# Scores of two attention groups as three fp32r products of high parts and rests, in an encoder layer on one core

## The chip, the cores and the metric

The kernel runs on one core of one Trainium2 chip. The metric is the device time of one execution in microseconds. The kernel before takes 909.24 us, the median of three runs (908.89, 909.24 and 909.37).

## What is computed

One encoder layer over 512 positions of width 1024: a LayerNorm, a mixer of two groups of attention heads, a cross attention to a memory of 256 rows, and a gated feed-forward block, each followed by a residual sum and a LayerNorm. The change touches the mixer only. Cut to it, the reference reads:

```python
def banded_attention(q, k, v, n_side, sink=None):
    ...
    s = jnp.einsum('bnqhgd,bnkhd->bnhgqk', qb, kw).astype(jnp.float32) * (dh ** -0.5)
    ...
    p = jnp.where(mask, jnp.exp(s - m[..., None]), 0.0)
    ...
def parallel_mixer(h, positions, w_in, attn_sink, g_win, g_dil, w_out):
    z = h @ w_in
    qa, ka, va, qb, kb, vb = jnp.split(z, SPLITS, axis=-1)
    qa = partial_rope(qa...); ka = partial_rope(ka...)
    out_a, _ = banded_attention(qa, ka, va, WIN_HALF, attn_sink.reshape(WIN_KV_HEADS, -1))
    ...
    for gi, (window, dil) in enumerate(DIL_PAIRS):
        o, lse = banded_attention(to_residue(qb[:, :, gi], dil), to_residue(kb[:, :, gi], dil), ...)
```

The eight **sink heads** (`qa`, `ka`, `va`) have a window of 128 on each side, an extra sink logit, and only two key heads. The second group has eight heads in each of three dilations (`DIL_PAIRS` is (128, 1), (512, 4), (2048, 16)); its member with dilation 1 is the **undilated group**. Every head is 64 wide, so a score product contracts over 64 rows.

## The kernel before

**Products.** All large products take fp32 data apart: a high part, which is the number cast to fp32r by ScalarE (ACT), and a rest, which VectorE (DVE) gets by subtracting the high part from the number. TensorE (PE) then adds three products, high by high, high by rest and rest by high. `wsplit` (lines 134 to 142) does that for a block of weights: the cast is L136, the subtraction L138. The scores of the mixer are the exception. They are products of plain fp32 numbers, which PE takes in two passes, so that each shows as two records in the trace.

**Two heads at once.** A tile of queries or keys holds two heads, on partitions 0 to 63 and 64 to 127 (`HJ`). Score products are issued for the two heads in turn, `j` = 0 and 1; each uses one half of the rows of PE's array.

**Projections.** `proj` makes 512 positions of two heads: 24 matmuls of 512 columns into a PSUM tile `g` (`chunk_fm`), then the rotation (`rope`, lines 525 to 531). That is a product (L528) and a shuffle (L529) on DVE, then a product (L530) and a sum (L531) on GpSimd (POOL). The sum writes the tile of queries or keys, in fp32. Such tiles come from a pool of 12 buffers of 2 KB a partition (tag `x`).

**Items.** The attention itself runs as items between the projections. `item_a(c)` is the undilated group for heads 2c and 2c+1 (called A0 to A3 here), `item_w(c)` the sink heads (W0 to W3), `item_b(c)` the other two dilations (B0 to B3). An item issues its score products on PE, then for each block and head a masked minimum on DVE (L725, L771 or L815) and an exponential on ACT (L728, L774 or L819), both in that order on their engines. It pauses, transposes the probabilities on PE (L682), lets ACT copy them out of PSUM (L687), pauses, and multiplies them by the values (L694).

**Order.** PE's order is the program's own (`manual_schedule`): a counter `now` goes up by one for each matmul of a projection (`mmt`, `tick`), and an item goes on once its keys and queries are `ready` and its pause is over. `proj` sets `ready` to `now + LAG`, and `LAG` is 24 matmuls. Item A's transposes come 18 matmuls behind its scores. If no buffer of the pool is free, `x_tile` forces the next item. The order of ACT, DVE and POOL is set by the compiler's scheduler when the kernel is built. Each engine then works through its own list in that order.

Of the kernel before, what the change touches and what calls it, by code (L numbers as in the profile page):

```python
# [9 lines left out]
F32 = mybir.dt.float32  # L10
F32R = mybir.dt.float32r
I32 = mybir.dt.int32
AF = mybir.ActivationFunctionType
ALU = mybir.AluOpType
# [3 lines left out]
P = 128  # L18
D = 1024
S = 512  # L20
# [17 lines left out]
QA, KA, VA, QB, KB, VB = 0, 512, 640, 768, 2304, 3840  # L38
# [34 lines left out]
def hymba_layer(ctx: ExitStack, tc: tile.TileContext, A, cst_d, out):  # L73
    nc = tc.nc
# [11 lines left out]
    xpool = ctx.enter_context(pool("x2k", side="right"))  # L86
# [3 lines left out]
    rope = [cpool.tile([P, S], F32, tag="rope", bufs=2, name=n) for n in ("rc", "rsn")]  # L90
# [43 lines left out]
    def split(raw, shape, hp, htag, hb, lp, ltag, lb, eng=None):  # L134
        hi = hp.tile(shape, F32R, tag=htag, bufs=hb, name="hi")
        nc.scalar.copy(hi, raw)  # L136
        lo = lp.tile(shape, F32R, tag=ltag, bufs=lb, name="lo")
        (eng or nc.vector).tensor_tensor(lo, raw, hi.bitcast(F32), ALU.subtract)  # L138
        return hi, lo
# [4 lines left out]
    def w_cols(w, c0, eng=None):  # L144
        raw = wpool.tile([P, KD, P], F32, tag="raw", bufs=3, name="raw")
        nc.sync.dma_start(raw, w.rearrange("(k p) f -> p k f", p=P)[:, :, c0 : c0 + P])
        return wsplit(raw, [P, KD, P], eng)
# [19 lines left out]
    def mm(o, l, r, first, last):  # L167
        on_pe(nc.tensor.matmul(o, l, r, start=first, stop=last))  # L168
# [91 lines left out]
    def v_raw(i):  # L260
        src = w_in[2 * i * P : (2 * i + 2) * P, VB : VB + 512].rearrange("(k p) f -> p k f", p=P)
        if i < 3:
            raw = [wpool.tile([P, 2, 512], F32, tag="raw", bufs=3, name="raw")]
            nc.sync.dma_start(raw[0], src)
        else:
            raw = [xpool.tile([P, 1, 512], F32, tag="x", bufs=12, name="raw") for _ in range(2)]
            for k in range(2):
                nc.sync.dma_start(raw[k], src[:, k : k + 1, :])
        wv0.append([raw, [wpool.tile([P, 2, 512], F32R, tag=n, bufs=6, name=n) for n in ("hi", "lo")]])
# [255 lines left out]
    def rope(ps, view, dest):  # L525
        rn[0] += 1
        zc, sh = zs[:, rn[0] % 2, :], zs[:, 2 + rn[0] % 2, :]
        nc.vector.tensor_tensor(zc, ps, rc, ALU.mult)  # L528
        nc.vector.stream_shuffle(sh, ps, SWAP)  # L529
        nc.gpsimd.tensor_tensor(sh, sh, rsn, ALU.mult)  # L530
        nc.gpsimd.tensor_tensor(view[1](dest), view[0](zc), view[0](sh), ALU.add)  # L531
# [8 lines left out]
    m2 = cst[:, CM1 + 64 : CM1 + 192]  # L540
    mB = cst[:, CM1 : CM1 + 384].rearrange("p (a b) -> p a b", b=192)[:, :, 64:192]
    mA = cst[:, CMA : CMA + 384]
    ka = p1.tile([P, S], F32, name="ka")
    sq = ka
    va = p1.tile([P, NB, P], F32, name="va")
    Q = {}
    V = {0: vt}
# [31 lines left out]
        while any(q[0] == name for q in queue):  # L579
            force()  # L580

    XB = 12

    def x_tile(shape, dt, key):
        while sum(e[1] for e in held) >= XB:
            force()
        t = xpool.tile(shape, dt, tag="x", bufs=XB, name="x")
        held.append([key, True])
        return t

    def x_free(*keys):
        for e in held:
            if e[0] in keys:
                e[1] = False

    def mmt(o, l, r, first, last, w=1.0):
        mm(o, l, r, first, last)
# [12 lines left out]

    def proj(key, wt, view, dest=None):
        ps = chunk_fm(key, wt)
        if dest is None:
            dest = Q[key] = x_tile([P, S], F32, key)
        rope(ps, view, dest)
        ready[key] = now[0] + LAG

    def proj_b(n, g, c):
        wt = first.pop(n) if g == c == 0 else w_cols(w_in, (KB if n == "k" else QB) + g * 512 + c * P)
# [71 lines left out]
    def pv(o, parts):  # L691
        for i, (t0, t1, lhs, rhs) in enumerate(parts):
            for j in range(2):
                nc.tensor.matmul(  # L694
                    o[HJ[j], t0:t1], lhs(j), rhs(j), start=i == 0, stop=i == len(parts) - 1
                )

    def item_a(c):
        k, q = Q["k", 0, c], Q["q", 0, c]
        s = [s_tile() for _ in range(2)]  # L700
        cols = ((0, 0), (0, 128), (1, 0), (1, 256))
        for q0, o0, kk0 in ((0, 0, 0), (448, 64, 384)):
            for j in range(2):
                mm(s[j][o0 : o0 + 64, 0, 0:P], q[HJ[j], q0 : q0 + 64], k[HJ[j], kk0 : kk0 + P], True, True)
        for u in range(1, 4):
            bk, c0 = cols[u]
            for j in range(2):
                mm(
                    s[j][:, bk, c0 : c0 + 256],
                    q[HJ[j], 128 * u - 64 : 128 * u + 64],  # L710
                    k[HJ[j], 128 * (u - 1) : 128 * (u + 1)],
                    True,
                    True,
                )
        x_free(("k", 0, c), ("q", 0, c))
        pus = []
        for u in range(4):
            nk = 256 if u else P
            bk, c0 = cols[u]
            pu = p2.tile([P, 2, nk], F32, tag="p", bufs=4, name="pu")  # L720
            pus.append(pu)
            for j in range(2):
                h_ = 2 * c + j
                ng, dn = (stT[:, i, u, h_ : h_ + 1] for i in (0, 1))
                nc.vector.tensor_tensor_reduce(  # L725
                    pu[:, j, :], s[j][:, bk, c0 : c0 + nk], m1 if u else m2, SCALE, 3.0e38, ALU.add, ALU.min, ng
                )
                nc.scalar.activation(pu[:, j, :], pu[:, j, :], AF.Exp, bias=ng, scale=-1.0, accum_out=dn)  # L728
        yield 18
        lo = [pu[:, j, 0:P] for pu in pus for j in range(2)]  # L730
        up = [pu[:, j, P : 2 * P] for pu in pus[1:] for j in range(2)]
        t1, t2, t3, t4 = transposes(
            lo[0:4], [up[0], lo[4], up[1], lo[5]], [up[2], lo[6], up[3], lo[7]], [up[4], up[5]]
        )
        yield 13
        yield from meet()
        o = ps_tile("o", 1)

        def vj(kb):
            return lambda j: vt[:, kb, c * P + j * HD : c * P + (j + 1) * HD]  # L740

        pv(
            o,
            [
                (0, 64, vj(0), lambda j: t1[:, j, 0:64]),
                (64, 192, vj(0), lambda j: t1[:, 2 + j, :]),
                (192, 448, vj(2), lambda j: t3[:, 2 * j : 2 * j + 2, :]),
                (64, 320, vj(1), lambda j: t2[:, 2 * j : 2 * j + 2, :]),
                (320, 448, vj(3), lambda j: t4[:, j, :]),
                (448, 512, vj(3), lambda j: t1[:, j, 64:128]),  # L750
            ],
        )
        nc.scalar.copy(oA[:, c, :], o)

    def item_b(c, then=None):
# [35 lines left out]
        pv(o, [(u * P, (u + 1) * P, vj(g, u), pj(g, u)) for u in range(4) for g in (1, 2)])  # L791
        nc.scalar.copy(oB[:, c, :].rearrange("p (i r) -> p r i", r=4), o.rearrange("p (r i) -> p r i", r=4))

    def item_w(c, then=None):
        q = Q["w", c]
        st = spool.tile([P, NB, 2], F32, tag="ast", bufs=2, name="ast")
# [5 lines left out]
        pu4 = [p2.tile([P, 2, 386], F32, tag="p", bufs=4, name="pu") for _ in range(NB)]  # L802
        for b in (0, 3, 1, 2):
            k0, k1 = max(0, b - 1) * P, min(NB, b + 2) * P
            for j in range(2):
                mm(sc[b][j][:, 0 : k1 - k0], q[HJ[j], b * P : (b + 1) * P], ka[HJ[j], k0:k1], True, True)
        x_free(("w", c))
        for b in (0, 3, 1, 2):
            nk = (min(NB, b + 2) - max(0, b - 1)) * P
# [60 lines left out]
        nc.vector.tensor_tensor(oW[:, c, :], o, fw, ALU.mult)  # L870
        if c < 3:
            return
        for i in range(4):
            if i == 0:
                nc.scalar.activation(sq, oW[:, i, :], AF.Square)
            else:
                tmp = p2.tile([P, S], F32, tag="p", bufs=4, name="tmp")
                nc.scalar.activation(tmp, oW[:, i, :], AF.Square)
                nc.vector.tensor_tensor(sq, sq, tmp, ALU.add)
# [38 lines left out]
    def rms_scale(sq_, name):  # L918
        ps = ps_tile("o", 1, [P, NB, 2])
        for b in range(NB):  # L920
            mm(ps[:, b, :], sq_[:, b * P : (b + 1) * P], ones, True, True)
        ra = spool.tile([P, NB], F32, tag=name, bufs=1, name=name)
        nc.vector.tensor_scalar(ra, ps[:, :, 0], 1.0 / 512, EPS, ALU.mult, ALU.add)
        nc.gpsimd.tensor_tensor(ra, ra, mhalf.to_broadcast([P, NB]), ALU.pow)
        return ra
# [10 lines left out]
    with tc.manual_schedule(engines={nc.tensor.engine}):  # L936
# [6 lines left out]
        proj_b("k", 0, 0)  # L943
        proj_b("q", 0, 0)
        add("A0", keys_a(0), item_a(0))
        proj(("ka",), w_cols(w_in, KA), NAT, ka)
        proj_va()
        add("W0", [("w", 0), ("ka",)], item_w(0))
        proj_w(0)
# [36 lines left out]
        def item_c():  # L986
# [25 lines left out]
            tp = ps_tile("t", 1, [P, 4, P])  # L1012
            for u in range(4):
                nc.tensor.transpose(tp[:, u, :], stw[:, u].rearrange("p n h -> p (n h)"), ident)
            hp["w"] = rms_scale(sq, "raw_")
            for c in range(4):
                split_gain(mT, c, oW[:, c, :], gwc[:, c : c + 1])
            xw, rr = (cs.tile([8, 2, S], F32, tag="n4", bufs=2, name=n) for n in ("xw", "rr"))
# [356 lines left out]

    def t_parts(n, i, r):
        if n < 3:
            hl = [xpool.tile([P, 2, HT], F32R, tag="x", bufs=12, name="x") for _ in range(2)]
        else:
            hl = [two_k(t4, i), cpool.tile([P, 2, HT], F32R, tag="rope", bufs=2, name="t4l")]  # L1380
        nc.scalar.copy(hl[0], r)
        nc.vector.tensor_tensor(hl[1], r, hl[0].bitcast(F32), ALU.subtract)
        T.setdefault(n, []).append(hl)
# [101 lines left out]
    with gs:  # L1485
# [18 lines left out]

        def down_ops(k):
            w = w_rows(A["w_down"][0], k, 1, 0, D)
            a = split(act[:, k, :], [P, S], xpool, "x", 12, xpool, "x", 12)
            return w, a

        for k in range(KO):  # L1510
# [78 lines left out]
```

## Time and profile before

| what | before |
|---|---|
| median of three runs | 909.24 us |
| the profiled execution | 910.02 us |
| its span, first to last instruction | 908.2 us |
| around the span | 1.8 us |
| granted TensorE clock | 0.998 |
| PE busy | 896.0 us (99%) |
| DVE, ACT, POOL busy | 562.1, 385.5, 127.3 us |
| the mixer's projections and items | from about 41 to 340 us of the span |

A row of the timeline gives start and length in microseconds, engine, line and operation, the tile written and the tiles read, and in square brackets how long the engine sat idle before it and what ended that. A row of the chain of waits gives start and length of a stretch that belongs to the chain which ended last. Lengths on PE contain the way through the array, so the time that a matmul takes in a row of others is read from start to start.

### The profile page before, as it was taken

How to read it: one execution, taken by the hardware profiler on the slowest of the kernel's cores; microseconds unless marked ns; L12 is line 12 of the kernel's file. 1: busy time of each engine (PE TensorE's matmuls, PEld its weight loads, DVE VectorE, ACT ScalarE, POOL GpSimd, SP SyncE). 2: the span in 40 equal slices, each digit the busy share in tenths (PEclk: the TensorE clock that was granted, in tenths of full speed). 3: DMA queues.
4: the chain of work that ended last, by engine and by line, in shares of the span. 5: the costliest groups of instructions: out<-in, count | busy, mean ns of one | idle time of the engine just before them, and what ended most of it. 6: DMA issues, size and time to landing. Idle time of an engine off the chain costs nothing.

```text
span 908.2 us, 12950 instructions
## 1 busy us (share of the span) xinstructions
PE 896.0 (99%) x5115; PEld 768.8 (85%) x5115; DVE 562.1 (62%) x963; ACT 385.5 (42%) x672; POOL 127.3 (14%) x106
## 2 busy tenths in 40 slices
PE   8999999999999999999999999999999999999996
PEld 6778987898878798788988889899999999888885
DVE  6975145335446767869366576977777767433357
ACT  4573436415546576415454224444444445222210
POOL 1064033431443420010000010000000000000001
PEclk9999999999999999999999999999999999999999
DMA  6762041224221338415222304333333354223201
GB/s 218 224 216 70 24 140 47 71 69 117 70 71 47 93 109 237 142 47 167 89 70 70 90 26 121 91 93 93 97 112 93 95 161 140 93 94 102 83 23 70
DMA packets 117086, 92.84 MB, mean 102 GB/s; under 512 B 12488, under 2 KB 101024, under 8 KB 117026
## 3 DMA queue, kind: packets, MB, share of 16 engines
q1 hardware_dynamic: 116192, 89.80, 32.7%
q10 hardware_dynamic: 834, 2.22, 0.6%
q8 instruction: 40, 0.66, 0.3%
q14 instruction: 20, 0.16, 0.1%
HBM read 87.82 MB, written 4.19 MB: 101 GB/s over the span
## 4 chain that ended last, share of the span: by engine, by line
PE 95%; DVE 3%; DMA 1%; issue 0%; ACT 0%; POOL 0%; DVEq 0%; ACTq 0%
PE g L168 53%; PE s L168 25%; PE o L168 5%; PE t L168 4%; PE o L694 3%; PE s L682 2%; PE s L208 1%; DMA vt<-in_ln_in_g_dram 1%; PE s L1225 0%; DVE lo L282 0%; DVE oA L348 0%; DVE st L312 0%; DVE Tlo L367 0%; POOL zs L530 0%; DVE mx L1206 0%
## 5 line engine op out<-in xcount | busy, mean ns | idle before, releaser
L138 DVE TENSOR_TENSOR lo<-raw,hi 128x1024 fp32r<-128x1024 f32 x126 | 157.3, 1249 | 87.8 <-ACT hi L136 87.1
L136 ACT CAST hi<-raw 128x1024 fp32r<-128x1024 f32 x126 | 132.3, 1050 | 141.1 <-PE g L168 92.5
L168 PE MATMUL g<-Thi,hi 128*128 128x512 f32 x240 | 94.8, 395 | 0.0
L168 PE MATMUL g<-Tlo,hi 128*128 128x512 f32 x240 | 94.3, 393 | 0.0
L168 PE MATMUL g<-Thi,lo 128*128 128x512 f32 x240 | 94.0, 392 | 0.0
L109 POOL TENSOR_TENSOR rs<-ve,mhalf 128x1 f32<-128x1 f32 x18 | 15.3, 853 | 523.5 <-DVE ve L115 512.2
L530 POOL TENSOR_TENSOR zs<-zs,rsn 128x512 f32<-128x512 f32 x29 | 59.2, 2041 | 147.5 <-DVE zs L529 147.5
L168 PE MATMUL g<-Uhi,hi 128*128 128x512 f32 (+1 forms) x216 | 74.3, 344 | 0.0
L168 PE MATMUL g<-Ulo,hi 128*128 128x512 f32 (+1 forms) x216 | 74.0, 342 | 0.0
L168 PE MATMUL g<-Uhi,lo 128*128 128x512 f32 (+1 forms) x216 | 73.9, 342 | 0.0
L168 PE MATMUL g<-hi,Thi 128*128 128x512 f32 x184 | 71.6, 399 | 0.0
L168 PE MATMUL g<-hi,Tlo 128*128 128x512 f32 x184 | 71.0, 395 | 0.5 <-DVE Tlo L1173 0.5
L168 PE MATMUL g<-lo,Thi 128*128 128x512 f32 x184 | 70.6, 395 | 0.4 <-DVE lo L282 0.4
L528 DVE TENSOR_TENSOR zs<-g,rc 128x512 f32<-128x512 f32 x29 | 20.0, 688 | 68.5 <-PE g L168 31.7
L168 PE MATMUL g<-x,hi 128*128 128x256 f32 x320 | 58.8, 284 | 0.0
L168 PEld LDWEIGHTS g<-Thi,hi 128*128 128x128 f32 x240 | 45.1, 188 | 11.0 <-issue 0.9
L168 PEld LDWEIGHTS g<-Tlo,hi 128*128 128x128 f32 x240 | 45.1, 188 | 10.3 <-issue 1.4
L168 PEld LDWEIGHTS g<-Thi,lo 128*128 128x128 f32 x240 | 45.1, 188 | 9.3
L168 PEld LDWEIGHTS g<-x,hi 128*128 128x128 f32 x320 | 50.0, 192 | 0.5 <-issue 0.3
L168 PE MATMUL s<-Uhi,hi 128*128 128x512 f32 (+1 forms) x136 | 49.5, 364 | 0.0
L168 PE MATMUL s<-Ulo,hi 128*128 128x512 f32 (+1 forms) x136 | 49.5, 364 | 0.0
L168 PE MATMUL s<-Uhi,lo 128*128 128x512 f32 (+1 forms) x136 | 49.5, 364 | 0.0
(369 smaller groups left out, 2059.5 us busy)
## 6 DMA issues: line engine op xcount, KB each, us to landing
raw<-in_w_in_dram SPq DMA_DIRECT2D x37, 512.0 KB, 3.7
raw<-in_w_gate_dram SPq DMA_DIRECT2D x22, 512.0 KB, 3.8
raw<-in_w_up_dram SPq DMA_DIRECT2D x22, 512.0 KB, 3.9
raw<-in_w_down_dram SPq DMA_DIRECT2D x22, 512.0 KB, 3.4
raw<-in_w_xk_dram SPq DMA_DIRECT2D x8, 512.0 KB, 3.9
raw<-in_w_xv_dram SPq DMA_DIRECT2D x8, 512.0 KB, 3.5
raw<-in_w_xq_dram SPq DMA_DIRECT2D x8, 512.0 KB, 4.5
raw<-in_w_xo_dram SPq DMA_DIRECT2D x8, 512.0 KB, 3.5
```

The costliest lines, as they stand in the source:

```text
L109: nc.gpsimd.tensor_tensor(out_, in_, mhalf, ALU.pow)
L136: nc.scalar.copy(hi, raw)
L138: (eng or nc.vector).tensor_tensor(lo, raw, hi.bitcast(F32), ALU.subtract)
L168: on_pe(nc.tensor.matmul(o, l, r, start=first, stop=last))
L208: on_pe(nc.tensor.transpose(ps[:, i // 4, f : f + P], t[:, i * P : (i + 1) * P], ident))
L528: nc.vector.tensor_tensor(zc, ps, rc, ALU.mult)
L530: nc.gpsimd.tensor_tensor(sh, sh, rsn, ALU.mult)
L682: nc.tensor.transpose(tp[:, k, :], s_, ident)
L694: nc.tensor.matmul(o[HJ[j], t0:t1], lhs(j), rhs(j), start=i == 0, stop=i == len(parts) - 1)
```

## The change

The queries and keys of the sink heads and of the undilated group (13 projections: k and q of A0 to A3, the sink heads' key tile `ka`, and the four sink query tiles) are taken apart, as weights are. The new `in_parts` does it: ACT casts the rotated tile to a high part (new L600), DVE subtracts it for the rest (new L601). The new `scores` adds three fp32r products where one fp32 product stood. For these projections `ready` is 8 matmuls later. Each now holds two tiles instead of one, and one more while it is taken apart, so the pool has 18 buffers; to make room, the scratch for dynamic DMAs is set to 1 KB. At the edges of the sequence, item A issued two products of 64 queries each, which lay side by side in one PSUM tile. It now issues a product of 128 queries (384 to 511), of which the first 64 rows are then written over by a product of 64 queries (0 to 63). The other dilations (item B) keep their fp32 scores.

```diff
-    ka = p1.tile([P, S], F32, name="ka")
-    sq = ka
+    kfill = p1.tile([P, 32], F32, name="kfill")
+    kaT = [p1.tile([P, S], F32R, tag=n, bufs=1, name=n) for n in ("kah", "kal")]
...
-    XB = 12
+    XB = 18
...
+    PAIRS = ((0, 0), (0, 1), (1, 0))
+
+    def in_parts(raw, hl):
+
+        nc.scalar.copy(hl[0], raw)
+        nc.vector.tensor_tensor(hl[1], raw, hl[0].bitcast(F32), ALU.subtract)
...
     def proj(key, wt, view, dest=None):
         ps = chunk_fm(key, wt)
-        if dest is None:
-            dest = Q[key] = x_tile([P, S], F32, key)
-        rope(ps, view, dest)
-        ready[key] = now[0] + LAG
+        if view is RES:
+            Q[key] = x_tile([P, S], F32, key)
+            rope(ps, view, Q[key])
+            ready[key] = now[0] + LAG
+            return
+        raw = x_tile([P, S], F32, "raw")
+        rope(ps, view, raw)
+        Q[key] = dest or [x_tile([P, S], F32R, key) for _ in range(2)]
+        in_parts(raw, Q[key])
+        x_free("raw")
+        ready[key] = now[0] + LAG + 8
...
+    def scores(out_, q, q0, q1, k, k0, k1):
+        for i, (m, n) in enumerate(PAIRS):
+            for j in range(2):
+                mm(out_[j], q[m][HJ[j], q0:q1], k[n][HJ[j], k0:k1], i == 0, i == 2)
...
-        for q0, o0, kk0 in ((0, 0, 0), (448, 64, 384)):
-            for j in range(2):
-                mm(s[j][o0 : o0 + 64, 0, 0:P], q[HJ[j], q0 : q0 + 64], k[HJ[j], kk0 : kk0 + P], True, True)
+        scores([s[j][:, 0, 0:P] for j in range(2)], q, 384, 512, k, 384, 512)
+        scores([s[j][0:64, 0, 0:P] for j in range(2)], q, 0, 64, k, 0, P)
         for u in range(1, 4):
             bk, c0 = cols[u]
...
+            scores([s[j][:, bk, c0 : c0 + 256] for j in range(2)], q, 128 * u - 64, 128 * u + 64, k, 128 * (u - 1), 128 * (u + 1))
...
-            for j in range(2):
-                mm(sc[b][j][:, 0 : k1 - k0], q[HJ[j], b * P : (b + 1) * P], ka[HJ[j], k0:k1], True, True)
+            scores([sc[b][j][:, 0 : k1 - k0] for j in range(2)], q, b * P, (b + 1) * P, kaT, k0, k1)
...
-    nc = bacc.Bacc("TRN2", target_bir_lowering=False, num_devices=1)
+    nc = bacc.Bacc("TRN2", target_bir_lowering=False, num_devices=1, dynamic_dma_scratch_size=1024)
```

The rest of the diff gives the pool its 18 buffers where later stages take tiles of it, and puts the sum of squares `sq`, which used the memory of `ka`, into that of `kah`.

The scheduler lays the new work on ACT and DVE between the old. First place: ACT around A0, the first item. Before, four casts of weights (`hi`) stand ahead of the load of the table for exponentials and A0's first exponential (L728):

```order
L136 CAST hi<-raw 128x1024
L372 DMA h_dram<-oW 128x1024
L136 CAST hi<-raw 128x1024 x2
L728 ACT_TABLE_LOAD
L728 ACTIVATE pu,stT<-pu,stT 128x128
L728 ACTIVATE pu,stT<-pu,stT 128x256 x3
```

Now, with the high parts of k and q of A0 (both `x`) and of the sink heads' keys (`kah`); A0's exponentials are L739:

```order
L136 CAST hi<-raw 128x1024
L372 DMA h_dram<-oW 128x1024
L600 CAST x<-x 128x512
L136 CAST hi<-raw 128x1024
L600 CAST x<-x 128x512
L136 CAST hi<-raw 128x1024
L600 CAST kah<-x 128x512
L739 ACT_TABLE_LOAD
L739 ACTIVATE pu,stT<-pu,stT 128x128
L739 ACTIVATE pu,stT<-pu,stT 128x256
```

The cast of `kah`, which A0 does not read, stands ahead of the table load and of all of A0's exponentials.

Second place: DVE at the same point. Before, from the shuffle of A0's q on, the rotation of `ka` (the second L528) follows with only a weights' rest ahead of it:

```order
L529 STREAM_SHUFFLE zs<-g 128x512
L138 TENSOR_TENSOR lo<-raw,hi 128x1024
L528 TENSOR_TENSOR zs<-g,rc 128x512
L529 STREAM_SHUFFLE zs<-g 128x512
L138 TENSOR_TENSOR lo<-raw,hi 128x1024
L725 ISA pu,stT<-s,cst 128x128
```

Now the rests of k and q (L601) stand between:

```order
L529 STREAM_SHUFFLE zs<-g 128x512
L601 TENSOR_TENSOR x<-x 128x512
L138 TENSOR_TENSOR lo<-raw,hi 128x1024
L601 TENSOR_TENSOR x<-x 128x512
L528 TENSOR_TENSOR zs<-g,rc 128x512
L529 STREAM_SHUFFLE zs<-g 128x512
L138 TENSOR_TENSOR lo<-raw,hi 128x1024
L736 ISA pu,stT<-s,cst 128x128
```

So the rotation of `ka` begins behind the rest of q.

Third place: DVE around B1, where the sink queries of W3 have just been projected. Before, the rotation (L528, L529), a weights' rest, the scaling of W2's result (L870) and B1's first masked minimum (L771):

```order
L528 TENSOR_TENSOR zs<-g,rc 128x512
L529 STREAM_SHUFFLE zs<-g 128x512
L138 TENSOR_TENSOR lo<-raw,hi 128x1024
L870 TENSOR_TENSOR oW<-o,fw 128x512
L771 ISA pu,stT<-s,cst 128x256
```

Now, with the same steps under their new line numbers:

```order
L528 TENSOR_TENSOR zs<-g,rc 128x512
L529 STREAM_SHUFFLE zs<-g 128x512
L138 TENSOR_TENSOR lo<-raw,hi 128x1024
L882 TENSOR_TENSOR oW<-o,fw 128x512
L601 TENSOR_TENSOR x<-x 128x512
L782 ISA pu,stT<-s,cst 128x256
```

The rest of W3's queries, which B1 does not read, stands ahead of B1's minima; on ACT its cast stands likewise ahead of B1's exponentials.

More of the change, by code (lines that the diff above doesn't have):

```diff
@@ L265, in v_raw @@
         else:
-            raw = [xpool.tile([P, 1, 512], F32, tag="x", bufs=12, name="raw") for _ in range(2)]
+            raw = [xpool.tile([P, 1, 512], F32, tag="x", bufs=18, name="raw") for _ in range(2)]
             for k in range(2):
@@ L701, in item_a @@
         cols = ((0, 0), (0, 128), (1, 0), (1, 256))
-        for q0, o0, kk0 in ((0, 0, 0), (448, 64, 384)):
-            for j in range(2):
-                mm(s[j][o0 : o0 + 64, 0, 0:P], q[HJ[j], q0 : q0 + 64], k[HJ[j], kk0 : kk0 + P], True, True)
+        scores([s[j][:, 0, 0:P] for j in range(2)], q, 384, 512, k, 384, 512)
+        scores([s[j][0:64, 0, 0:P] for j in range(2)], q, 0, 64, k, 0, P)
         for u in range(1, 4):
             bk, c0 = cols[u]
-            for j in range(2):
[L708 to L714, printed above, removed]
+            scores([s[j][:, bk, c0 : c0 + 256] for j in range(2)], q, 128 * u - 64, 128 * u + 64, k, 128 * (u - 1), 128 * (u + 1))
         x_free(("k", 0, c), ("q", 0, c))
@@ L792, in item_b @@
         nc.scalar.copy(oB[:, c, :].rearrange("p (i r) -> p r i", r=4), o.rearrange("p (r i) -> p r i", r=4))
+    sq_ = []
     def item_w(c, then=None):
@@ L804, in item_w @@
             k0, k1 = max(0, b - 1) * P, min(NB, b + 2) * P
-            for j in range(2):
-                mm(sc[b][j][:, 0 : k1 - k0], q[HJ[j], b * P : (b + 1) * P], ka[HJ[j], k0:k1], True, True)
+            scores([sc[b][j][:, 0 : k1 - k0] for j in range(2)], q, b * P, (b + 1) * P, kaT, k0, k1)
         x_free(("w", c))
@@ L872, in item_w @@
             return
+        sq = p1.tile([P, S], F32, tag="kah", bufs=1, name="sq")
+        sq_.append(sq)
         for i in range(4):
@@ L945, in hymba_layer @@
         add("A0", keys_a(0), item_a(0))
-        proj(("ka",), w_cols(w_in, KA), NAT, ka)
+        proj(("ka",), w_cols(w_in, KA), NAT, kaT)
         proj_va()
@@ L1014, in item_c @@
                 nc.tensor.transpose(tp[:, u, :], stw[:, u].rearrange("p n h -> p (n h)"), ident)
-            hp["w"] = rms_scale(sq, "raw_")
+            hp["w"] = rms_scale(sq_[0], "raw_")
             for c in range(4):
@@ L1377, in t_parts @@
         if n < 3:
-            hl = [xpool.tile([P, 2, HT], F32R, tag="x", bufs=12, name="x") for _ in range(2)]
+            hl = [xpool.tile([P, 2, HT], F32R, tag="x", bufs=18, name="x") for _ in range(2)]
         else:
@@ L1506, in down_ops @@
             w = w_rows(A["w_down"][0], k, 1, 0, D)
-            a = split(act[:, k, :], [P, S], xpool, "x", 12, xpool, "x", 12)
+            a = split(act[:, k, :], [P, S], xpool, "x", 18, xpool, "x", 18)
             return w, a
```

## The prediction

> **What bounds the kernel now.** I read the page's busy times and the shares of the chain of waits first.
>
> ```profile
> PE 896.0 (99%) x5115; PEld 768.8 (85%) x5115; DVE 562.1 (62%) x963; ACT 385.5 (42%) x672; POOL 127.3 (14%) x106
> q1 hardware_dynamic: 116192, 89.80, 32.7%
> PE 95%; DVE 3%; DMA 1%; issue 0%; ACT 0%; POOL 0%; DVEq 0%; ACTq 0%
> ```
>
> PE is the bound: 95% of the chain is its own. Two things can then move the time: PE's own work, and new gaps in it. A gap of 1 us on PE between 41 and 340 us costs 1 us, because behind it PE is busy to the end.
>
> Next I read the chain in order of time, around the items.
>
> ```profile
> 57.10 1.95 PE s L168 x20
> 59.05 4.31 PE g L168 x18
> 63.36 1.53 PE s L682 x14
> ...
> 149.61 1.71 PE s L168 x12
> 151.96 7.94 PE g L168 x34
> ...
> 212.38 1.99 PE s L168 x32
> ...
> 257.13 1.99 PE s L168 x32
> 259.12 4.35 PE g L168 x18
> 263.47 1.75 PE s L682 x16
> ...
> 401.38 5.44 PE g L168 x24
> ...
> 425.84 5.76 PE g L168 x48
> ```
>
> The first three rows are A0: scores, 18 matmuls of a projection, 14 transposes in 1.53 us, 0.109 each. 149.61 is W1 (part of its scores go to other tiles, so its time is up to 151.96, 2.35 us), 212.38 and 257.13 are B0 and B1. The last two rows are plain fp32r streams: 0.227 us a matmul of 512 columns and 0.120 of 256.
>
> **PE's own work.** How long an fp32 score takes stands in the timeline of W0.
>
> ```profile
> 81.00 0.48 PE L168 MATMUL t<-ka,x 64*128 64x384 f32 x1
> 81.00 0.48 PE L168 MATMUL o<-ka,x 64*128 64x384 f32 x1
> 81.32 0.48 PE L168 MATMUL t<-ka,x 64*128 64x384 f32 x1
> ```
>
> The two heads start together (`t` and `o`), and the second pass 0.32 us later. So a step, both heads side by side, takes 0.32 at 384 columns, and by columns 0.215 at 256. W has two pairs of each width in two passes: 4 x 0.215 + 4 x 0.32 = 2.14. The other 0.21 of its 2.35 go to changing the array's shape, and stay. After: three fp32r products in place of two passes. From 0.120 and 0.227, 384 columns take 0.174; 6 x 0.120 + 6 x 0.174 = 1.76. W saves 0.38, four of them 1.5.
>
> A's three inner blocks take 3 x 2 x 0.215 = 1.29 now and 9 x 0.120 = 1.08 after. Its edges are four matmuls of 128 columns that run four at a time in two passes. A step of 128 columns takes (1.99 - 0.21) / 16 = 0.111 in B0, so the edges take 0.22. After: 3 steps for 128 queries, 3 for 64. No row shows fp32r at 128 columns; between half of 0.120 and all of it, I take 0.112 for the first (nearest: the same width in fp32) and 0.09 for the second, 0.61 together, and 0.1 for one more change of shape (bounds 0 and 0.21). Edges +0.49, inner blocks -0.21: +0.28, four of them +1.1. PE's own work: -1.5 + 1.1 = **-0.4 us**. Bounds: with 0.113 and 0.170 per step, half-price edges and no shape change, -2.3; with full-price edges and 0.21, +0.5.
>
> All this supposes that fp32r products of two heads also run side by side. In the trace fp32r runs on all 128 rows or, for `sel`, on one half only. I take the nearest row, the fp32 pair above, and keep the opposite as a rival. The Trainium skill, "TensorEngine Tiling (Array Packing)", Tiling Modes, says that tiles on different rows work independently, and that a change of tiling mode drains the array: by the first the sum is the -0.4, against it the rival's +13.4; by the second the extra shape change in A is paid in full, +0.4 in all. The trace agrees for fp32; no row shows fp32r.
>
> **Thirteen casts and thirteen rests.** They have the shape of these groups:
>
> ```profile
> L138 DVE TENSOR_TENSOR lo<-act,hi 128x512 fp32r<-128x512 f32 x22 | 14.8, 689 | 50.6 <-ACT hi L136 50.6
> L136 ACT CAST hi<-act 128x512 fp32r<-128x512 f32 x22 | 13.4, 622 | 62.5 <-PE s L168 62.4
> ```
>
> 13 x 0.62 = 8.1 us on ACT and 13 x 0.69 = 9.0 on DVE, engines that are busy 42% and 62%. Their lengths cost nothing; their places in the lists do. An item's exponentials can stand behind a cast that waits for a rotation which the item does not need. Here is A0: ACT, DVE and POOL.
>
> ```profile
> 56.66 1.05 ACT L136 CAST hi<-raw 128x1024 fp32r<-128x1024 f32 x1 [4.39 <-PE g L168]
> 57.72 1.28 ACT L728 ACT_TABLE_LOAD   x1
> 59.63 0.40 ACT L728 ACTIVATE pu<-pu,stT 128x128 f32<-128x128 f32 x1 [0.62 <-DVE stT L725]
> ...
> 62.88 0.49 ACT L728 ACTIVATE pu<-pu,stT 128x256 f32<-128x256 f32 x1
> ```
>
> ```profile
> 56.94 0.69 DVE L528 TENSOR_TENSOR zs<-g,rc 128x512 f32<-128x512 f32 x1 [2.40 <-issue]
> ```
>
> ```profile
> 55.76 1.28 POOL L531 TENSOR_TENSOR x<-zs 128x512 f32<-128x512 f32 x1
> 58.36 2.18 POOL L530 TENSOR_TENSOR zs<-zs,rsn 128x512 f32<-128x512 f32 x1 [1.32 <-DVE zs L529]
> 60.62 1.29 POOL L531 TENSOR_TENSOR ka<-zs 128x512 f32<-128x512 f32 x1
> ```
>
> The exponentials take 62.88 + 0.49 - 59.63 = 3.74 and end at 63.37, just as the transposes begin at 63.36: **no slack**. Step by step, after:
>
> - q's sum on POOL ends at 57.04; cast +0.62 and rest +0.69 with two handovers: 58.4.
> - The rotation of `ka`, at 56.94 before, stands behind that rest on DVE and starts at about 58.4, 1.45 later. So its sum on POOL ends at 61.91 + 1.45 = 63.4.
> - The cast of `kah` ends at 64.0, the table load at 65.3, the last exponential at 69.05.
> - PE: 8 matmuls more ahead of A0 are 1.8 us, so A0 starts about 58.55 (its wait for POOL in 57.10, some 0.3 us, goes) and takes 1.95 + 0.28; then 4.31 of projection: transposes from 65.1, to 66.6 if nothing held them. The last three need the last exponential: 69.05 + 0.33 = 69.4.
>
> PE stands still for **2.8 us**. If POOL's product runs in 1.3 us instead of 2.18, it is 1.9; if its sum is as slow as its product, 3.7.
>
> The same at B1:
>
> ```profile
> 254.92 0.69 DVE L528 TENSOR_TENSOR zs<-g,rc 128x512 f32<-128x512 f32 x1 [2.98 <-POOL x L531]
> ...
> 259.15 0.42 DVE L771 CUSTOM_DVE_ANT_1 pu<-s,cst 128x256 f32<-128x256 f32 x1 [1.18 <-PE s L168]
> ```
>
> ```profile
> 258.58 1.28 POOL L531 TENSOR_TENSOR x<-zs 128x512 f32<-128x512 f32 x1
> ```
>
> ```profile
> 259.68 0.51 ACT L774 ACTIVATE pu<-pu,stT 128x256 f32<-128x256 f32 x1 [4.00 <-DVE stT L771]
> ...
> 263.14 0.49 ACT L774 ACTIVATE pu<-pu,stT 128x256 f32<-128x256 f32 x1
> ```
>
> W3's rotation ends on POOL at 259.86; cast and rest end at 261.2, and only then do B1's minima start, 2.05 later than 259.15. The last exponential ends at 263.63 + 2.05 = 265.7, the transposes behind it at 266.0 instead of 263.47 + 1.75 = 265.2: **0.8 us** (0 to 1.9).
>
> W0 and W1 have more room: their exponentials are followed by a copy (L831) that PE needs at L845.
>
> ```profile
> 87.19 0.62 ACT L831 COPY x<-rd 128x512 f32<-128x512 f32 x1 [0.27 <-DVE rd L829]
> ```
>
> ```profile
> 92.05 0.44 PE o L845 x4
> ```
>
> That is 4.2 us of room. The cast of the next q now stands ahead of this copy, and its rotation ends only some 11 us behind W's start at 79.4; with cast and copy 12.2, against 92.05 - 79.4 = 12.7, less the 0.38 saved. Together with A2, whose minima are cut by one rest, I take **0.4 us** (0 to 1.0). Weight casts that now stand behind a cast of queries lose up to 3 us; the 4.39 of idle time at 56.66 says that they come that far ahead of PE's need, so this costs nothing. SP's and ACT's DMAs move with them, under the same cover. Only hardware queues appear among the DMAs, q1 with 89.80 MB above all, and DMA is 1% of the chain, at its start; so I price the smaller scratch and the six more buffers at nothing. Later stages keep PE's order.
>
> The Trainium skill, "TensorE: Matmul & The Clock Gate", opening table, gives ScalarE and VectorE a queue of 8 that is strictly first in, first out. By this rule the 2.8 and 0.8 are due; if ACT could take an exponential past a waiting cast they would be 0, and the sum -0.3. The trace agrees: the cast at 56.66 waits 4.39 us, and the table load behind it, which needs nothing, starts only at 57.72.
>
> **The sum.** -0.4 for PE's work, -0.3 for the wait ahead of A0, +2.8, +0.8 and +0.4 for the gaps: +3.3. On the profiled execution, 910.02, it gives 913.3; on the median of the runs, 909.24, which is 0.8 lower, **912.5 us**.
>
> **The rivals.**
> - *No pairs.* fp32r products of two heads run one after the other. W takes 12 x 0.120 + 12 x 0.174 = 3.53 against 2.14, A 18 x 0.120 and 6 x 0.112 + 6 x 0.09 + 0.1 against 1.51: (1.39 + 1.96) x 4 = 13.4. A0's exponentials then get 1.7 us more time, so the gaps are 2.3. 909.24 + 13.4 + 2.3 - 0.3 = 924.6. For it: no row shows fp32r on both halves. Against: fp32 starts both in the same hundredth of a microsecond (81.00), on the same halves. Chance 0.13.
> - *fp32r at 128 columns is as slow as fp32*, two passes of 0.111: A's edges take 6 x 0.222 instead of 0.61, +0.7 four times: 915.4. No row speaks against it. Chance 0.10.
> - *No gaps: not slower.* The place is the cast of `kah`. If the rotation of `ka` is done by the time A0's scores end, the exponentials start as early relative to the transposes as before, and a B1 that is as lucky loses nothing either. Then -0.7 is left, 908.5; with the low end of PE's work 906.6. It decides where POOL's sum for `ka` ends before about 60.6 (2.8 us earlier than I reckon). For it: POOL's pace varies (2.18 and 1.28 for like work). Against: the order on ACT and the time at which `ka`'s projection ends on PE, 56.9. Chance 0.20.
> - *The change doing less than it says* is not to be had: the new products and casts are in the lists. What is left, 0.07, is spread on both sides.
>
> **How the numbers follow.** The forecast has 0.50. Its own bounds: PE -2.3 to +0.5, gaps 1.9 to 6.6, less 0.3: 908.5 to 916.0. The range takes in the 128-column rival and most of the rival without gaps: **908.4 to 916.5**. Left out are the pairless case and tails, about 0.19. Chances, with 0.2% (1.8 us) about what a measurement of this kernel can tell from no change: slower, 0.45 of the forecast's 0.50, 0.13 and 0.10: 0.68. Same: 0.05 of the forecast, 0.13 of the gapless case, 0.03 of the rest: 0.21. Faster: 0.11.
>
> **What would show it.** On the chain, a row of DVE, ACT or POOL between A0's scores and its transposes, and ACT's table load near 65 instead of 57.7. In the timeline of W0, two heads' fp32r records starting together, with steps near 0.120 and 0.174, W some 0.4 shorter and A some 0.3 longer. B1's minima some 1.3 to 2 us behind its scores. I am wrong if heads start one after the other, if A's transposes follow 4.3 us behind its scores, or if PE gets gaps behind 340 us.

## The result, and the profile after

| what | before | after |
|---|---|---|
| median, six runs of each side by side | 909.59 us | 914.19 us |
| the profiled execution | 910.02 us | 914.18 us |
| its span | 908.2 us | 912.4 us |
| granted TensorE clock | 0.998 | 0.997 |

The change makes the kernel slower by 4.6 us: the ratio is 1.0054, with a 95% interval from 1.0041 to 1.0066. The prediction was 912.5 us, slower, with a range from 908.4 to 916.5.

The page of the changed kernel, busy times and shares of the chain of waits:

```profile
PE 898.5 (98%) x5187; PEld 772.2 (85%) x5187; DVE 575.5 (63%) x976; ACT 390.9 (43%) x685; POOL 124.6 (14%) x106
PE 85%; DVE 6%; POOL 3%; ACT 3%; issue 2%; DMA 1%; DVEq 0%; ACTq 0%; POOLq 0%
```

PE's share of the chain fell from 95% to 85%. The other engines' work that now stands in it isn't all lost time, since the chain can pass through an engine while PE is busy beside it. The lost time is where PE stands still. Here is the chain in order of time (start, length, what) around A0:

```profile
57.01 0.68 DVE x L601
57.69 0.54 DVE zs L528
...
59.03 2.19 POOL zs L530
...
61.29 1.29 POOL x L531
...
62.61 0.62 ACT kah L600
...
63.25 1.28 ACT L739
...
64.54 1.04 ACT pu L739 x5
...
65.73 0.69 ACT pu L739 x3
...
66.46 2.87 PE s L696 x11
```

Read it backwards from the transposes (L696): they wait for A0's exponentials, these for the load of ACT's table, this for the cast of `kah`, this for the rotation of `ka` on POOL and DVE, and the rotation for the rest of q. A0's transposes need neither `kah` nor `ka`.

DVE's list has the same pattern. The rest of `kah` stands ahead of the last four of A0's eight minima:

```profile
63.26 0.69 DVE L601 TENSOR_TENSOR kal<-x,kah 128x512 fp32r<-128x512 f32 x1 [2.10 <-ACT kah L600]
63.87 0.42 DVE L736 CUSTOM_DVE_ANT_0 pu<-s,cst 128x256 f32<-128x256 f32 x1
```

Here it is covered: the fifth minimum ends at 64.29, and ACT, which starts late behind the table load and then works without a pause, comes to the fifth exponential only at 66.31. So the cast ends last.

B1, in the same view:

```profile
261.78 1.29 POOL x L531
...
263.09 0.63 ACT x L600
...
263.75 0.69 DVE x L601
264.44 0.34 DVE pu L782
...
265.88 1.58 ACT pu L785 x6
...
267.50 2.03 PE s L696 x15
```

B1's first minimum (L782) comes behind the rest of W3's queries, and its last transposes behind the exponentials.

The new scores of W0 on PE, in the timeline:

```profile
85.42 0.34 PE L168 MATMUL s<-kah,x 64*128 64x384 f32 x2
85.59 0.33 PE L168 MATMUL t<-kah,x 64*128 64x384 f32 x1
85.59 0.33 PE L168 MATMUL o<-kah,x 64*128 64x384 f32 x1
```

The two heads' fp32r products (`t` and `o`) start in the same hundredth of a microsecond, and a step of 384 columns takes 85.59 - 85.42 = 0.17 us.

A table of stretches, each read from the start of its first matmul on PE to the start of the next stretch's first, shows where the 4.6 us are. "In all" means the sum over four items. The stretches that aren't listed have the length they had, but that some projection matmuls move from one to another.

| stretch | before | after | difference |
|---|---|---|---|
| wait for POOL or DVE just ahead of A0's scores | 0.3 | 0 | -0.3 |
| scores of A, each of four | 1.88 | 1.79 | -0.4 in all |
| scores of W, each of four | 2.36 | 1.97 | -1.5 in all |
| A0, from its scores' end to its product with the values (with one projection matmul less, 0.23 us, after) | 9.04 | 12.98 | +4.2 |
| W0, transposes to product with the values | 6.14 | 6.48 | +0.3 |
| A2, from its scores' end to the transposes' end | 5.67 | 6.40 | +0.7 |
| W1, as W0 | 5.92 | 6.44 | +0.5 |
| B1, transposes | 1.66 | 2.78 | +1.1 |

The sum is +4.6 (4.7 from unrounded rows). Behind the mixer nothing is added. In the two profiled executions PE is only 4.0 us behind at 345 us and 4.2 at the end, because the kernel after began its first product into a tile `g` 0.7 us earlier (at 6.32, before at 7.02), far ahead of the mixer. Over the twelve profiles of this case that start lies anywhere between 5.81 and 7.30, so the 0.7 is not put down to the change.

The gap at A0 has a second part, which the chain does not show. In this row a stretch of time is followed by its length, the busy time of PE, PE's weight loads, DVE, ACT and POOL, the granted clock, and the DMAs' share and rate:

```profile
66.65:70.06 3.41, 3.41 (x14) 2.31 (x14) 2.62 (x6) 3.41 (x11) 2.00 (x4) 0.50 0.00 0
```

At the end of the gap PE ran at half its clock for 3.41 us. The next projection began at 68.98, so its first 1.08 us ran at half clock and lost some 0.5 us: its 13 matmuls took 3.66 us, against 3.16 in the run below that makes the keys' parts on POOL and has no gap at A0 (granted clock 1.00 in the same stretch).

### The profile page after: what moved, and what is told of

Its sections match the earlier page's. It is cut to its first block, busy times and chain, and to the rows that moved or that the text cites. A ratio compares the mean times of both kernels' runs of the same rounds, so it can differ in the third digit from the quotient of the medians.

```text
span 912.4 us, 13099 instructions
## 1 busy us (share of the span) xinstructions
PE 898.5 (98%) x5187; PEld 772.2 (85%) x5187; DVE 575.5 (63%) x976; ACT 390.9 (43%) x685; POOL 124.6 (14%) x106
## 4 chain that ended last, share of the span: by engine, by line
PE 85%; DVE 6%; POOL 3%; ACT 3%; issue 2%; DMA 1%; DVEq 0%; ACTq 0%; POOLq 0%
PE g L168 46%; PE s L168 24%; PE o L168 5%; PE t L168 4%; PE o L708 2%; PE s L696 2%; POOL zs L530 2%; POOL x L531 1%; DVE lo L138 1%; PE s L208 1%; DVE zs L529 1%; ACT hi L136 1%; DVE pu L827 1%; ACT pu L785 1%; ACT pu L739 0%
## 5 line engine op out<-in xcount | busy, mean ns | idle before, releaser
L138 DVE TENSOR_TENSOR lo<-raw,hi 128x1024 fp32r<-128x1024 f32 x126 | 161.7, 1285 | 97.3 <-ACT hi L136 96.6
L136 ACT CAST hi<-raw 128x1024 fp32r<-128x1024 f32 x126 | 132.2, 1050 | 129.0 <-PE g L168 70.5
L530 POOL TENSOR_TENSOR zs<-zs,rsn 128x512 f32<-128x512 f32 x29 | 54.3, 1873 | 149.7 <-DVE zs L529 143.5
L168 PEld LDWEIGHTS g<-hi,Tlo 128*128 128x128 f32 x184 | 42.2, 230 | 6.6 <-DVE Tlo L1187 1.0
```

## The experiments

Ratios are to the kernel before in runs on the same chip, with their 95% intervals. Fences of changed lines are cut at "...".

**Room alone.** The kernel before with the new pool and scratch:

```diff
-    XB = 12
+    XB = 18
...
-    nc = bacc.Bacc("TRN2", target_bir_lowering=False, num_devices=1)
+    nc = bacc.Bacc("TRN2", target_bir_lowering=False, num_devices=1, dynamic_dma_scratch_size=1024)
```

> The kernel before with 18 buffers in place of 12 and the scratch of 1 KB, nothing taken apart, scores in fp32. Theory (the casts and rests, by their places in the lists of ACT and DVE, make the gaps): no difference, ratio to the kernel before 0.999 to 1.001, 909.6 us. Rival (room: more buffers let work be issued earlier and collide, or the small scratch costs): part or all of the 4.6 us is here, ratio 1.002 to 1.005.

Measured: 909.62 against 909.70 us, ratio 0.9997 (0.9988 to 1.0006). Buffers and scratch cost nothing; the loss is not there.

**Casts without the new products.** The changed kernel with fp32 scores:

```diff
-        for i, (m, n) in enumerate(PAIRS):
-            for j in range(2):
-                mm(out_[j], q[m][HJ[j], q0:q1], k[n][HJ[j], k0:k1], i == 0, i == 2)
+        for j in range(2):
+            mm(out_[j], q[0][HJ[j], q0:q1].bitcast(F32), k[0][HJ[j], k0:k1].bitcast(F32), True, True)
...
```

> All 13 casts and 13 rests and the later readiness stay as in the changed kernel, but the scores are fp32 products of the high parts alone, in the shapes of before (the rests are computed and not used, so the scores lack the terms with them). Theory: PE's own work is that of before and the gaps are those of the change, near 6.3 us together, so 915.6 us, ratio 1.006 to 1.007, A0's transposes again some 3.5 us late. Rival (the gaps come from the new products, their weights or their shapes): gaps gone, 909.3 us, ratio 1.000.

Measured: 921.92 us, the median of only four runs (919.65 to 922.73), ratio 1.0135 (1.0120 to 1.0151). The gaps stay without the new products, so the rival is out; but the loss is twice what I expected. At A0, ACT's timeline has the pattern of the change with fp32 scores:

```profile
62.91 0.62 ACT L600 CAST kah<-x 128x512 fp32r<-128x512 f32 x1 [4.98 <-POOL x L531]
63.55 1.28 ACT L738 ACT_TABLE_LOAD   x1
```

The table load comes 5.26 us behind the start of A0's scores (58.29), in the change 5.37. This kernel's chain of waits shows what is added:

```profile
58.82 7.14 DMA oB<-in_mem_dram
...
65.99 0.69 DVE st L131
66.68 0.19 DVE pu L735
...
68.40 0.94 ACT hi L136
...
99.29 1.27 POOL x L531
100.58 0.62 ACT x L600
101.20 0.53 ACT x L842
```

The scheduler laid the lists anew. At A0, DVE's fifth minimum (L735) now stands behind a statistic (L131) of the cross attention's memory, which waits for a DMA, and a cast of weights (L136) stands ahead of the last exponential. At W0, the copy that PE needs (L842) stands behind the cast of A1's queries, which waits for their rotation: W0's transposes take 4.96 us in place of 2.18. B1's transposes take 2.78 us, as in the change, with fp32 scores. So the casts' places make the gaps, and their size is the scheduler's accident. As in the change, the granted clock falls to 0.50 for 3.41 us at the end of A0's gap (from 69.65). The four runs spread with their mean clock (919.65 us at 0.995, 921.55 at 0.994, 922.29 and 922.73 at 0.992); only the fastest was profiled, so where the others lost clock is not known.

**The keys' parts on POOL.** One cast and one rest moved, PE's order the same row by row:

```diff
-        in_parts(raw, Q[key])
+        if key == ("ka",):
+            nc.gpsimd.tensor_copy(Q[key][0], raw)
+            nc.gpsimd.tensor_tensor(Q[key][1], raw, Q[key][0].bitcast(F32), ALU.subtract)
+        else:
+            in_parts(raw, Q[key])
```

> The changed kernel with one cast and one rest moved: the high part and the rest of the sink heads' keys are made by POOL instead of ACT and DVE; PE's order is the same, row by row. Theory (kah's cast ahead of A0's exponentials makes the gap at A0): table load near 58 us, A0's transposes 4.2 to 4.6 us behind its scores, gap of 3.65 us gone but for 0.3, so 910.9 us, ratio to before 1.001 to 1.002. Rival (the gap comes from q's rest on DVE ahead of the rotation, and from later readiness, and stays when the cast goes): 914.2 us, ratio 1.005.

Measured: 910.75 us, ratio 1.0011 (1.0003 to 1.0020). ACT's timeline and the chain of waits of this kernel at A0:

```profile
58.19 1.28 ACT L743 ACT_TABLE_LOAD   x1
60.87 0.41 ACT L743 ACTIVATE pu<-pu,stT 128x128 f32<-128x128 f32 x1 [1.39 <-DVE stT L740]
```

```profile
58.55 1.79 PE s L168 x27
60.34 4.33 PE g L168 x18
64.67 1.53 PE s L700 x14
```

The table load is at 58.19, and PE goes from scores to transposes without another engine in the chain. The rest of q still stands ahead of the rotation of `ka` on DVE here, and PE's order and the readiness are those of the change, so the rival is out: the parts of `kah` in the lists of ACT and DVE make the whole gap at A0. Cast and rest moved together, so that it was the cast which ended last is read from the trace of the change. The granted clock stays at 1.00 here. The other stretches keep what they had (W0 +0.3, A2 +0.7, W1 +0.5, B1 +1.1).

**Sink queries on POOL too.** The same for the four sink query tiles, which get 8 matmuls more before they are ready:

```diff
+        if key[0] in ("ka", "w"):
...
-        ready[key] = now[0] + LAG + 8
+        ready[key] = now[0] + LAG + (16 if key[0] == "w" else 8)
```

> The changed kernel with the high parts and rests of the sink heads' keys and of all four sink query tiles made by POOL, and the sink queries ready 8 matmuls later than in the change. Theory: the gap at A0 goes as with the keys alone, that at B1 (1.1 us) too, and those at W0, W1 and A2 (1.6 us) at least in half; PE's own work stays 1.9 us less than before: 908.8 us, ratio to before 0.998 to 1.000. Rival (POOL at 1.3 to 2.2 us for each pass becomes late itself, and slows DVE meanwhile): W's scores wait for it, 911 us or more, ratio 1.002 or more.

Measured: 909.46 us, ratio 0.9996 (0.9988 to 1.0005): some 0.7 us above what I expected. B1 (1.66 for its transposes) and A2 are as before. But W1's transposes took 2.64 as in the change, and W0's 3.35 us, more than in the change (2.49) and not the half that I expected. In ACT's timeline the copy that W0's last transposes need starts at 94.45, behind the cast of A1's queries at 93.44, which waited 2.74 us for their rotation. The gaps that come from parts of sink queries go with these; what is left at W0 stands behind a cast of A's.

**One half of the change at a time.** First the undilated group alone (`ka` and the sink queries stay fp32):

```diff
-        if view is RES:
+        if key == ("ka",):
+            rope(ps, view, dest)
+            ready[key] = now[0] + LAG
+            return
+        if view is RES or key[0] == "w":
...
```

> Only the undilated group is taken apart; the sink heads keep their fp32 tiles and scores. Theory: no cast of kah ahead of A0's exponentials and no split of W3's queries at B1, so no gap at A0 and B1; A saves 0.4 and the wait ahead of A0 0.3, and the casts of A's keys and queries that stand near W0, W1 and A2 cost 0.3 to 1.6: 909.2 to 910.5 us, ratio 1.000 to 1.001. Rival (q's rest and the later readiness make the gap at A0): 912.5 to 913.2 us, ratio 1.003 to 1.004.

Measured: 909.29 us, ratio 0.9993 (0.9984 to 1.0001). No gap at A0, and the scheduler's lists gave none at W0, W1 or A2 either, though A's casts are all on ACT: the same casts can stand where they cost nothing. Then the sink heads alone:

```diff
-        if view is RES:
+        if view is RES or key[0] in "kq":
...
```

> Only the sink heads are taken apart; the undilated group keeps its fp32 tiles and scores. PE saves 1.5. Here the scheduler puts kah's cast behind three of A0's eight exponentials, and ka's rotation no longer stands behind q's rest; kah's cast ends near 62.6, five exponentials follow, so A0's transposes are late by 0.7 to 1.2. B1's minima still stand behind the rest of W3's queries: 1.1. Theory: 909.7 - 1.5 + 1.0 + 1.1 + 0 to 0.4 = 910.3 to 910.7 us, ratio 1.001. Rival (the whole gap at A0 belongs to kah's cast wherever it stands): 913 us, ratio 1.004.

Measured: 910.98 us, ratio 1.0013 (1.0004 to 1.0022). ACT's timeline at A0:

```profile
59.52 0.50 ACT L747 ACTIVATE pu<-pu,stT 128x256 f32<-128x256 f32 x1
60.94 0.62 ACT L600 CAST kah<-x 128x512 fp32r<-128x512 f32 x1 [0.83 <-POOL x L531]
```

Here the same cast waits 0.83 us, behind three exponentials, and A0's transposes lose 0.56 us (2.01 against 1.45). The rest of the loss is B1 (2.77 in place of 1.66) and A2, whose transposes take 2.41 in place of 1.45; that 0.96 is more than the 0.4 that I allowed for, so the time is a little above the range that I gave. So it is not the cast but its place that costs. The halves alone give -0.5 and +1.2 us, +0.7 between them, and together 4.6. Most of the difference is A0, where in the change `kah`'s cast stands ahead of the table load and `ka`'s rotation behind q's rest; why the scheduler places the cast so was not tested.

**Faster versions.** The sink heads alone, with POOL making their parts, so that ACT and DVE get no new work:

```diff
-        in_parts(raw, Q[key])
+        nc.gpsimd.tensor_copy(Q[key][0], raw)
+        nc.gpsimd.tensor_tensor(Q[key][1], raw, Q[key][0].bitcast(F32), ALU.subtract)
...
+        ready[key] = now[0] + LAG + (16 if key[0] == "w" else 8)
```

> Only the sink heads are taken apart, and POOL makes their high parts and rests; the lists of ACT and DVE hold what they held before. Theory: no gap at all but PE's saving of 1.5: 908.1 us, ratio to before 0.998 to 0.999. Rival (POOL's extra work delays the rotations or slows DVE, so that gaps come back): 909.5 us or more, ratio 1.000.

Measured: 908.09 us, ratio 0.9979 (0.9970 to 0.9988), 0.2% faster than before. Every stretch but W's scores has the length it had before. The same with less time for POOL:

```diff
-        ready[key] = now[0] + LAG + (16 if key[0] == "w" else 8)
+        ready[key] = now[0] + LAG + (11 if key[0] == "w" else 8)
```

> As the run with the sink heads alone in parts, made by POOL, but the sink queries are ready 11 instead of 16 matmuls later than an fp32 tile, since POOL's cast took only 0.61 us. Theory (there were no gaps left, so when an item starts does not matter): 908.1 us, ratio 0.998. Rival (POOL needs the time): W's scores wait for the rest, up to 1 us at each of four, 909 to 912 us.

Measured: 908.27 us, ratio 0.9978 (0.9969 to 0.9987), the same. Then both groups, with POOL making all parts but those of A0's keys and queries:

```diff
+        if key[0] in ("ka", "w") or key[-1] > 0:
+            nc.gpsimd.tensor_copy(Q[key][0], raw)
+            nc.gpsimd.tensor_tensor(Q[key][1], raw, Q[key][0].bitcast(F32), ALU.subtract)
...
-        ready[key] = now[0] + LAG + 8
+        ready[key] = now[0] + LAG + (8 if key[-1] == "ka" or key[-1] == 0 and key[0] != "w" else 16)
```

The tiles of A1 to A3 are thus ready 8 matmuls later too.

> As the run with the sink heads' parts made by POOL, but POOL also makes those of the keys and queries of A1 to A3; ACT and DVE make only those of A0. Theory (the 1.6 us that were left at W0 and W1 come from casts of A's keys and queries on ACT): these go too, PE's own saving of 1.9 is left, 907.8 us, ratio to before 0.998. Rival (POOL's list becomes the one that items stand behind: 1.9 us more for each tile, and W's small copies queued behind it): 909.5 us or more, ratio 1.000 or above.

Measured: 908.86 us, ratio 0.9989 (0.9981 to 0.9998): 1 us short of the theory. W0's and W1's transposes took 2.72 us each in place of 2.18. ACT's timeline of this kernel at W0:

```profile
94.01 1.07 ACT L705 COPY pT<-s 128x512 f32<-128x512 f32 x2 [0.76 <-PE s L700]
94.97 0.63 ACT L847 COPY x<-rd 128x512 f32<-128x512 f32 x1
```

The copy for W's last transposes (L847) now stands behind two copies of transposed probabilities. Its tile is one of the pool `x`. So it got a buffer of its own:

```diff
-        rb = x_tile([P, NB, P], F32, ("rb", c))
+        rb = p1.tile([P, NB, P], F32, tag="rb", bufs=1, name="rb")
...
-    XB = 18
+    XB = 17
...
```

> As the run in which POOL makes all parts but A0's, with one edit: the tile rb, which the copy ahead of W's last transposes writes, gets a buffer of its own, and the pool 17 in place of 18. Theory (the 0.54 us that were left at each of W0 and W1 come from that copy standing on ACT behind two copies of transposed probabilities, because its tile waited for a buffer that POOL frees late): both gaps go, 907.8 us, ratio to before 0.998. Rival (they are due to POOL working beside DVE and ACT): they stay, 908.9 us, ratio 0.999.

Measured: 907.78 us, ratio 0.9973 (0.9963 to 0.9984), 2.05 us faster than the kernel before. The copy now comes first:

```profile
89.38 0.62 ACT L847 COPY rb<-rd 128x512 f32<-128x512 f32 x1 [0.36 <-DVE rd L845]
92.55 2.06 ACT L705 COPY pT<-s 128x512 f32<-128x512 f32 x4 [0.75 <-PE s L700]
```

Both gaps are gone (2.18 us for the transposes of each). What is left is about what PE's own work and the wait ahead of A0 give, 1.9 and 0.3 us by the table above.

## Why the prediction was right, step by step

**The direction and the cause were right.** The place, the chain through `kah`'s cast and the order of the links are those of the forecast. One run took `kah`'s parts out of the lists of ACT and DVE and the gap went; another showed it without the new products, and a third ruled out the pool and the scratch. Measured from the start of A0's scores, the last exponential ended 10.40 us later (by its row on ACT, 67.79 and 0.49 us long); the prediction gives 69.05 - 58.55 = 10.5.

**PE's own work: -0.4, measured -1.9.** This term was mis-sized, and all of it in A. W's -0.38 each came out as forecast, so did the steps at 256 and 384 columns and the two heads side by side. A was to be 0.28 longer and is 0.09 shorter. Rows of A0's scores after, each from a narrow window of PE's timeline:

```profile
58.05 0.45 PE L168 MATMUL s<-x 64*128 64x128 f32 x6
58.27 0.52 PE L168 MATMUL s<-x 64*64 64x128 f32 x8
58.39 0.51 PE L168 MATMUL s<-x 64*64 64x128 f32 x6
```

58.05 is the second step of 128 queries and 58.27 the first of 64, two steps later: 0.11 each, as assumed. 58.39 is the third step of 64 queries: 0.06 each, not 0.09. All of the edges take 0.57 (57.88 to the inner blocks at 58.45) with the change of shape at their start in it. The 0.1 for one more change of shape isn't there; at most 0.05 of it is in the first step of the inner blocks, which takes 0.17 (58.45 to 58.62) where the later ones take 0.12. Before, the edges took not 0.22 but 0.38:

```profile
57.26 1.78 PE L168 MATMUL s<-x 64*64 64x128 f32 x16
```

Their second pass began at 57.26, the inner blocks at 57.48, 0.22 later and not 0.11. I priced that change of shape at nothing when I worked out the kernel before. Of the 0.37 by which each A came out shorter than forecast, 0.11 is this, 0.10 the change of shape that I added after, and 0.09 the steps of 64 queries. The rest is in the inner blocks, which gained 0.28 and not 0.21: their first step took 0.32 before (57.48 to 57.80) and not 0.215.

The Trainium skill, "TensorEngine Tiling (Array Packing)", Tiling Modes, says that tiles on different rows work independently; the trace agrees, now for fp32r too (85.59 for both heads). Its rule that a change of tiling mode drains the array fits the 0.11 us that were lost before between 64*64 and 64*128. After, between the products of 128 and 64 queries, no such time shows (steps of 0.11 and 0.06), so there the measurement decides against the extra +0.4 in A that I worked out from this rule.

**The wait ahead of A0: -0.3**, measured -0.3.

**The gap at A0: +2.8 (1.9 to 3.7), measured +4.2**, outside its bounds. The exponentials came when I said. PE was ready earlier, since A0's scores were 0.44 us shorter than forecast, and stood still for that much longer, so at A0 the shorter scores gained nothing. From the last exponential's end to the next projection matmul it took 0.70 us, not 0.33, and the first three matmuls of that projection took 0.5 us more than in the run without the gap. Both lie in the 3.41 us at half clock, so some 0.9 of the 1.4 us that the forecast lacks go with a granted clock of 0.50, which I had not reckoned with. Only the two profiles with the long gap at A0 show this fall, that of the change and that with fp32 scores; in the other ten the clock is 1.00 all through the mixer. What sets it off was not tested.

**The gap at B1: +0.8 (0 to 1.9), measured +1.1.** The minima began 4.1 us behind the start of the scores, as worked out (264.36 against 260.26, the start of the scores).

**W0, W1 and A2: +0.4 (0 to 1.0), measured +1.6**, outside the bounds of this term. The chain of the change, at A2 and at W0 in turn:

```profile
145.16 0.63 ACT x L600
...
145.81 0.69 DVE x L601
146.50 0.07 DVE pu L736
```

```profile
92.75 0.95 ACT hi L136
...
93.72 2.15 DVE lo L138
95.87 0.12 DVE rd L841
...
96.02 0.63 ACT x L843
```

At A2, the cast and the rest of W1's queries stand ahead of a minimum, the pattern of B1, which I saw only as "cut by one rest". At W0, I priced the cast of queries; what came last was the reciprocal (L841) behind a weights' rest of 2.15 us, whose cast the scheduler had pushed between W0's exponentials. At W1 the copy that PE needs stood behind a weights' cast too (165.76, 1.05 us long), and that behind the cast of A3's queries. The prediction held that weight casts which are pushed back cost nothing because they come far ahead of PE's need. For their own product that holds; for what stands behind them it does not.

**The sum.** +4.2 + 1.1 + 1.6 - 0.3 - 1.9 = +4.7, against +3.3. Two errors stand against each other: the gaps came out 2.9 us larger, PE's work 1.5 us smaller than priced. That the total came so near is in part luck. The range was also wide, 8.1 us for a forecast change of 3.3, and a time without any change lay inside it.

**The rivals.** *No pairs* and *fp32r at 128 columns as slow as fp32* are refuted by the rows above. *No gaps* was to hold if POOL's sum for `ka` ended before 60.6; it ended at 61.29 + 1.29 = 62.58. With the gaps taken away the time is below the kernel before, as this rival gave it for PE's work (908.5, and 906.6 at the low end; the last version runs at 907.8).

The Trainium skill, "TensorE: Matmul & The Clock Gate", opening table, gives ACT and DVE a strictly first in, first out queue. The trace agrees: ACT stood idle for 5.01 us ahead of the cast of `kah`, and the table load, which needs nothing, came behind it at 63.25; without that cast it came at 58.19.

```profile
62.61 0.62 ACT L600 CAST kah<-x 128x512 fp32r<-128x512 f32 x1 [5.01 <-POOL x L531]
```

## What to carry to other kernels

When a change puts small work on an engine that is half idle, don't price its length but its place: find each new instruction that waits for a slow producer, and see what stands behind it in that engine's list and who needs that. If it stands ahead of something that PE waits for, give it to an engine on which nothing urgent stands behind it; here POOL, with more lead for its tiles and a buffer of its own for one copy, turned a loss of 0.54% into a gain of 0.27%. A gap can also cost more than its own length: here the clock was halved behind it. Read the row of every stretch that you price, also of the kernel before: a stretch reckoned from steps left out a change of the array's shape that the trace would have shown.

## What the runs showed of the hardware

- In the change, fp32r products of two heads on the two halves of the rows run side by side, at 0.06 us a step for 64 queries on 128 keys, 0.11 for 128 on 128, 0.12 at 256 columns and 0.17 at 384.
- The granted clock fell to 0.50 for 3.41 us in the change (66.65 to 70.06) and in the run with fp32 scores (69.65 to 73.06), both times behind A0's gap, in which PE had only A0's transposes to do. The gaps at B1 (1.1 us) and, with the sink heads alone, at A0 (0.56) show no such fall.
- POOL casts 128 by 512 numbers from fp32 to fp32r about as fast as ACT (0.61 against 0.62 us; 0.70 on average in the run with ten such casts of queries and keys), while its sums and products of that size take 1.3 to 2.4. From the last version:

```profile
61.92 0.61 POOL L629 CAST kah<-x 128x512 fp32r<-128x512 f32 x1
62.62 1.28 POOL L630 TENSOR_TENSOR kal<-x,kah 128x512 fp32r<-128x512 f32 x1
```

- A rest on DVE and a sum or product on POOL that run at the same time hold each other up; in these rows the one that starts later takes longer. In the change the rest of A0's keys runs while POOL rotates the queries (its product from 53.01, its sum from 54.38), that of the queries while POOL is idle:

```profile
53.50 1.36 DVE L601 TENSOR_TENSOR x<-x 128x512 fp32r<-128x512 f32 x1 [0.56 <-ACT x L600]
...
57.01 0.68 DVE L601 TENSOR_TENSOR x<-x 128x512 fp32r<-128x512 f32 x1
```

Both are the same operation on the same shape. It goes the other way too: a weights' rest that began at 58.86 took 1.20 us, and POOL's product for `ka`, begun beside it at 59.03, took 2.18 in place of 1.29. The overlaps are read from the trace; they weren't tested by themselves.
